# Seven block products for eight in the second MLP layer of a one-core encoder block

## The chip, the core and the metric

The kernel runs on one NeuronCore of one Trainium2 chip. The metric is the device time of one execution in microseconds (us): 1042.65 us before the change, the median of three runs (1041.05 to 1043.44). Times inside the kernel come from one profiled execution, counted from the first to the last instruction of the core. A difference of about 0.2% (2 us) is the least that a measurement of this kernel can tell from none.

The engines are named as in the profile: PE (TensorE) multiplies matrices and PEld is its weight load, DVE (VectorE) and ACT (ScalarE) work elementwise, POOL (GpSimd) works elementwise and issues DMAs, SP (SyncE) only issues DMAs. A matmul multiplies a stationary operand of up to 128x128 with a moving operand of up to 128x512 and adds into a bank of PSUM of 128 rows by 512 columns. SBUF is the core's on-chip memory.

## What is computed

One layer of a hybrid encoder for 512 tokens of 1024 numbers: three token mixers (gated convolution, RG-LRU, RWKV-7), a gated merge, an output projection, and then a two-layer MLP with a final normalisation. Only the MLP matters here (`rms_norm` divides each token by its root mean square and multiplies by a weight):

```python
h2 = rms_norm(x, norm2_g[l])
x = x + jnp.square(jax.nn.relu(h2 @ mlp_w1[l])) @ mlp_w2[l]
return rms_norm(x, final_g)
```

The first weight matrix is 1024 x 4096, the second 4096 x 1024. All inputs and outputs are float32.

## The kernel before

**Number format.** A matmul of the kernel takes operands of type fp32r (float32 of reduced precision). To keep float32's precision each operand is kept as two fp32r tiles: `hi`, the value cast to fp32r (ACT), and `lo`, the rest, `value - hi` (DVE). A product is three matmuls into one PSUM bank, written by `mm3` (L167): hi by hi, and the two mixed ones. The three have lines L168, L169 and L170 in the profile.

**Weights.** `load_w` (L133) loads one 128 x 1024 row tile of weights (512 KB) into a `raw` buffer by a DMA of SP (L136), then `split_w` makes `whi` (ACT, L147) and `wlo` (DVE, through the helper `tt`, L104). There are two `raw` buffers, and three each of `whi` and `wlo`. Everything in `load_w` has a priority that puts it ahead of its place in the code, so that weights are fetched and split early.

**First layer.** For each of the 32 row tiles `fi` of the hidden vector the loop at L978 multiplies the weights with `h2h`, `h2l` (the merged activations, 8 tiles of 128 x 512): 24 matmuls into one PSUM bank `p1`. ACT takes the relu into `r` (L983), DVE squares it, ACT casts it to `ah` (L991), DVE makes `al`. The root-mean-square factor of each token is not in there: squared relu lets it be taken out, so it is applied after the second layer. Beside the first two row tiles, `to_tokens` transposes the residual stream to token rows, writes it to the DRAM tensor `x2d` and collects each token's sum of squares in `ss2`.

**Second layer.** The eight PSUM banks hold the output, 4 tiles of 128 tokens by 2 halves of 512 columns (`acc`). For each row tile `fi`, `mlp2` adds, for each of the eight banks, the product of `ah`/`al` (128 tokens, stationary) and `whi`/`wlo` (512 columns, moving): 24 matmuls per row tile, 768 in all. The residual comes back from `x2d` in one DMA of 2 MB, issued by POOL together with the final norm's weights `fgt` (L1003, L1005) when the first layer's operands are free.

**End.** The last `NL` = 3 row tiles are done token tile by token tile, so that `last(i)` of one token tile runs beside the matmuls of the next: DVE scales the bank by the token's factor `sc2` and adds the residual (L1037, helper line L107), ACT squares and sums (L1039), a root (L1045) and a reciprocal give the final norm's factor, DVE and ACT scale the two halves, and SP and ACT issue the output DMAs.

**What sets the order.** Each engine runs its instructions in one fixed order. A scheduler makes it from the code's order and the priorities when the program is built; a buffer that is handed out again makes its writer wait for the last reader of the earlier use. No engine overtakes an instruction of its own that waits.

Of the kernel before, what the change touches and what calls it, by code (L numbers as in the profile page):

```python
# [18 lines left out]
P = 128  # L19
# [13 lines left out]
NL = 3  # L33
# [65 lines left out]
def block_kernel(ctx, tc, xt, win, par, mulr, sw, wout, w1, w2, fg, cst, eyes, out):  # L99
# [848 lines left out]

    fc = fill_chain()
# [10 lines left out]
    NA = 3 * NF // 4  # L960
    with tc.tile_pool(name="mw", bufs=2) as mw, \
            tc.tile_pool(name="ap", bufs=1) as apool, \
            ExitStack() as apool2:
        ahs = [apool.tile([P, NA, S], F32R, name="ah", align_bytes=ALM)]
        als = [apool.tile([P, NA, S], F32R, name="al", align_bytes=ALM)]
        ahl = lambda fi: (ahs[fi // NA][:, fi % NA], als[fi // NA][:, fi % NA])

        def mlp1(t, w, beside=None):
# [6 lines left out]
            if beside:  # L975
                drain(beside)

        for fi in range(NF):  # L978
            t = pp.tile([P, S], F32, tag="pp", name="p1")
            w = load_w(w1[fi])  # L980
            mlp1(t, w, to_tokens(fi) if fi < 2 else None)
# [3 lines left out]
            if fi == NA:  # L985
                xr_ctx.close()
                ap2 = apool2.enter_context(tc.tile_pool(name="ap2", bufs=1))
                ahs.append(ap2.tile([P, NF - NA, S], F32R, name="ah2", align_bytes=AL))
                als.append(ap2.tile([P, NF - NA, S], F32R, name="al2", align_bytes=AL))
            ahi, alo = ahl(fi)  # L990
            ac.copy(ahi, r)  # L991
            tt(alo, r, f(ahi), SUB)
# [3 lines left out]
        sc2 = cp.tile([P, 4], F32, name="sc2")  # L996
        tt(sc2, ss2[:, 0], ss2[:, 1], ADD)
        ts2(sc2, sc2, 1.0 / D, EPS, MUL, ADD)
        v.reciprocal(sc2, sc2)
        h2_ctx.close()  # L1000
        with tc.tile_pool(name="fin", bufs=1, side="right") as fin:
            xr = fin.tile([P, 4, D], F32, name="xr2")
            gp.dma_start(xr, x2d.rearrange("i p d -> p i d"))  # L1003
            fgt = fin.tile([P, D], F32, name="fgt")
            gp.dma_start(fgt, fg.to_broadcast([P, D]))  # L1005
            bank = lambda pool, tag: pool.tile([P, S], F32, tag=tag, name="acc")
            acc = [[bank(pc, "pu"), bank(pc, "pS")], [bank(pc, "py"), bank(pm, "pm")],
                   [bank(pm, "pm"), bank(pp, "pp")], [bank(pp, "pp"), bank(pp, "pp")]]

            def mlp2(fi, w, i, h):  # L1010
                ms = slice(i * P, (i + 1) * P)
                ahi, alo = ahl(fi)
# [4 lines left out]
            for fi in range(NF - NL):  # L1017
                w = load_w(w2[fi])
                for i in range(4):
                    for h in range(2):  # L1020
                        mlp2(fi, w, i, h)

            wl2 = [load_w(w2[fi]) for fi in range(NF - NL, NF)]

            def last(i):
# [3 lines left out]
                if i == 0:  # L1029
                    for d_ in range(NL - 1):  # L1030
                        for h in range(2):
                            mlp2(NF - NL + d_, wl2[d_], i, h)
                for h in range(2):
                    hs = slice(h * S, (h + 1) * S)
                    for d_ in range(NL - 1 if i == 0 else 0, NL):
                        mlp2(NF - NL + d_, wl2[d_], i, h)
                    stt(xr[:, i, hs], acc[i][h], sc2[:, i:i + 1], xr[:, i, hs], MUL, ADD)  # L1037
                    junk = fin.tile([P, S], F32, tag="fj", name="fj", bufs=2)
                    ac.activation(junk, xr[:, i, hs], AF.Square, accum_out=ss[:, h:h + 1])  # L1039
                    if h == 0:  # L1040
                        x0, x1 = xr[:, i, 0:S], xr[:, i, S:D]
                        o0 = x0 if i < 3 else fin.tile([P, S], F32, name="x3f")
                        (gp if i < 3 else v).tensor_tensor(out=o0, in0=x0, in1=fgt[:, 0:S], op=MUL)
                tt(sd[:, 0:1], ss[:, 0:1], ss[:, 1:2], ADD)
                ac.activation(sd[:, 1:2], sd[:, 0:1], AF.Sqrt, bias=epst[:, 0:1], scale=1.0 / D)  # L1045
                v.reciprocal(sd[:, 0:1], sd[:, 1:2])
                stt(x1, x1, sd[:, 0:1], fgt[:, S:D], MUL, MUL)
                sy.dma_start(out[i, :, S:D], x1)
                ac.activation(o0, o0, AF.Copy, scale=sd[:, 0:1])
                ac.dma_start(out[i, :, 0:S], o0)  # L1050

            for i in range(4):
                last(i)
# [75 lines left out]
```

## Time and profile before

| | before |
|---|---|
| time, median of 3 runs | 1042.65 us |
| span of the profiled execution, first to last instruction | 1039.6 us |
| granted TensorE clock, mean | 0.996 |
| first layer, first to last matmul start | 680.0 to 857.7 us |
| second layer, first to last matmul start | 857.9 to 1031.7 us |
| busy in the span: PE, PEld, DVE, ACT, POOL | 98%, 80%, 62%, 46%, 11% |
| DMA: moved, mean rate over the span | 145.23 MB, 140 GB/s |

The span is that of the one execution that was profiled; what lies around it (3.05 us to the median of the runs) is start and end of the program. The page gives each engine's busy time, the same in 40 slices of 26 us, the DMA queues, the chain of waits that ended last, and groups of equal instructions with their mean duration. Matmuls overlap by pipelining: one shows 389 ns from start to end, but the next begins some 0.23 us after it, and only that distance adds up to time.

### The profile page before, as it was taken

Reading aid. Unit: us, or ns where it says so; the run is one execution under the profiler, and the core shown is the slowest. Engines: PE = TensorE matmul, PEld = TensorE weight load, DVE = VectorE, ACT = ScalarE, POOL = GpSimd, SP = SyncE. Lnnn points to the kernel's source line nnn. Section 1 sums busy time; section 2 is a strip of 40 time slices with the busy share of each in tenths; the row PEclk is TensorE's granted clock in tenths of the full one; section 3 lists DMA queues with packets and bytes.
Section 4 is the critical chain, followed back from the end, with each engine's and each line's share of the span. In section 5 each row is a group of like instructions: output and inputs, shape, how many; then the busy total and the mean of one; then the engine's idle time right before and its main releaser. Section 6 shows DMA issues by size and latency. Waiting matters only on the chain. (4 is left out here: it accounts for less than half of the span.)

```text
span 1039.6 us, 15488 instructions
## 1 busy us (share of the span) xinstructions
PE 1021.4 (98%) x6180; PEld 831.5 (80%) x6180; DVE 648.4 (62%) x1087; ACT 480.6 (46%) x694; POOL 110.4 (11%) x180
## 2 busy tenths in 40 slices
PE   8999999999999999999999999999999999999997
PEld 5777877888878788888888778888888888888885
DVE  6997596599865875994567787564444442212224
ACT  7756453655544635556454444353443332221124
POOL 1013011202112112012222101010000000000001
PEclk9999999999999999999999999999999999999999
DMA  6344644734446346343997524443223335333232
GB/s 231 125 122 125 173 129 133 203 112 133 127 137 172 122 142 203 114 117 108 312 280 224 159 88 139 158 162 102 93 91 101 102 101 185 100 102 102 87 96 81
DMA packets 44504, 145.23 MB, mean 140 GB/s; under 512 B 6096, under 2 KB 9680, under 8 KB 43408
## 3 DMA queue, kind: packets, MB, share of 16 engines
q1 hardware_dynamic: 29472, 91.02, 27.6%
q0 software_dynamic: 14240, 52.18, 17.4%
q8 instruction: 48, 0.79, 0.3%
q10 hardware_dynamic: 720, 1.05, 0.3%
q14 instruction: 24, 0.20, 0.1%
HBM read 117.49 MB, written 26.74 MB: 139 GB/s over the span
## 5 line engine op out<-in xcount | busy, mean ns | idle before, releaser
L104 DVE TENSOR_TENSOR wlo<-raw,whi 128x1024 fp32r<-128x1024 f32 (+1 forms) x164 | 198.1, 1209 | 262.0 <-ACT whi L147 261.8
L147 ACT CAST whi<-raw 128x1024 fp32r<-128x1024 f32 (+1 forms) x164 | 170.0, 1037 | 320.8 <-PE acc L170 125.0
L168 PE MATMUL pp<-hh,whi 128*128 128x512 f32 x688 | 271.0, 394 | 0.4 <-DVE rs L107 0.4
L169 PE MATMUL pp<-hl,whi 128*128 128x512 f32 x688 | 270.1, 393 | 0.0
L170 PE MATMUL pp<-hh,wlo 128*128 128x512 f32 x688 | 269.2, 391 | 0.2 <-DVE wlo L104 0.2
L168 PEld LDWEIGHTS pp<-hh,whi 128*128 128x128 f32 x688 | 129.1, 188 | 28.8 <-DVE rs L107 0.8
L170 PEld LDWEIGHTS pp<-hh,wlo 128*128 128x128 f32 x688 | 129.2, 188 | 27.4 <-DVE wlo L104 0.6
L169 PEld LDWEIGHTS pp<-hl,whi 128*128 128x128 f32 x688 | 129.2, 188 | 26.3
L168 PE MATMUL p<-h2h,whi 128*128 128x512 f32 x256 | 100.4, 392 | 0.0
L170 PE MATMUL p<-h2h,wlo 128*128 128x512 f32 x256 | 99.7, 389 | 0.0
L169 PE MATMUL p<-h2l,whi 128*128 128x512 f32 x256 | 99.7, 389 | 0.0
L168 PE MATMUL acc<-whi,ah 128*128 128x512 f32 x256 | 99.6, 389 | 0.0
L169 PE MATMUL acc<-wlo,ah 128*128 128x512 f32 x256 | 99.6, 389 | 0.0
L170 PE MATMUL acc<-whi,al 128*128 128x512 f32 x256 | 99.6, 389 | 0.0
L170 PEld LDWEIGHTS p<-h2h,wlo 128*128 128x128 f32 x256 | 48.1, 188 | 10.1
L169 PEld LDWEIGHTS acc<-wlo,ah 128*128 128x128 f32 x256 | 48.1, 188 | 10.0
L170 PEld LDWEIGHTS acc<-whi,al 128*128 128x128 f32 x256 | 48.1, 188 | 9.9
L168 PEld LDWEIGHTS acc<-whi,ah 128*128 128x128 f32 x256 | 48.1, 188 | 9.9
L169 PEld LDWEIGHTS p<-h2l,whi 128*128 128x128 f32 x256 | 48.1, 188 | 9.7
L168 PEld LDWEIGHTS p<-h2h,whi 128*128 128x128 f32 x256 | 48.1, 188 | 9.6
L991 ACT CAST ah<-r 128x512 fp32r<-128x512 f32 x32 | 19.9, 623 | 43.3 <-DVE r L104 43.3
L104 DVE TENSOR_TENSOR al<-r,ah 128x512 fp32r<-128x512 f32 x32 | 22.1, 692 | 20.9 <-ACT ah L991 20.9
(308 smaller groups left out, 1343.7 us busy)
## 6 DMA issues: line engine op xcount, KB each, us to landing
raw<-in_win SPq DMA_DIRECT2D x88, 512.0 KB, 3.7
raw<-in_w SPq DMA_DIRECT2D x64, 512.0 KB, 3.5
ax<-axd POOLq DMA_DIRECT2D x8, 1024.0 KB, 9.6
axd<-AXt POOLq DMA_DIRECT2D x12, 512.0 KB, 7.4
bkd<-BKT POOLq DMA_DIRECT2D x4, 1024.0 KB, 14.0
raw<-in_wout SPq DMA_DIRECT2D x8, 512.0 KB, 3.6
bk<-bkd POOLq DMA_DIRECT2D x7, 512.0 KB, 11.8
swr<-in_sw SPq DMA_DIRECT2D x16, 128.0 KB, 2.9
```

The lines of the kernel that those rows point to most:

```text
L104: return v.tensor_tensor(out=o, in0=a, in1=b, op=op)
L147: ac.copy(hi[:, sl], raw[:, sl])
L168: pe.matmul(ps, wh, xh, start=start, stop=False)
L169: pe.matmul(ps, wh, xl, start=False, stop=False)
L170: pe.matmul(ps, wl, xh, start=False, stop=stop)
L991: ac.copy(ahi, r)
```

## The change

**Pairs.** Of the 32 row tiles of the second layer, 24 are taken as 12 pairs (`NPAIR`). A pair's contribution is a 2 x 2 block product: its two row tiles by the two halves of the tokens (256 each) on one side, its two row tiles by the two halves of the columns (512 each) on the other. Done directly it has eight block products. The new code uses Strassen's scheme in Winograd's form: seven block products, with sums and differences of blocks as operands. A block product is 6 matmuls (two token tiles by three). The 8 other row tiles stay as they were, grouped in four units of two.

**Stages.** The eight banks are now four pairs of banks `BX`, `BZ`, `BY`, `BW`, and the products come in three stages over the pairs, with weights loaded for each stage anew:
- Stage 1 (`prep1`): per pair one 512 KB load; DVE makes the difference `T` and two `wlo` halves, ACT two `whi` halves; 12 matmuls into `BX` and `BZ`. For the last 4 pairs (from `NPS` = 8 on) the activation operands are also split here (`a2`).
- Stage 2 (`prep2`): one 512 KB load; DVE makes `T` and `raw` anew, then `wlo`, `tl` and `a3l`, ACT `whi`, `th`, `a3h`; 18 matmuls into `BY`, `BW`, `BX`. Ahead of every third pair a unit of plain row tiles (`prep_plain`, one 512 KB load of two half rows) adds 24 matmuls.
- Stage 3 (`prep3`): two loads of 256 KB; DVE makes `raw` anew, `wlo`, `a2l`, ACT `whi`, `a2h`; 12 matmuls into `BZ` and `BX`. Ahead of every sixth pair a plain unit of 24. The last two units are done token tile by token tile, 12 matmuls each, with `finish(i)` in the place of `last(i)`.

Between the stages `fold` adds a finished bank to the residual tile `xr` (DVE); a bank may go on accumulating after a fold, so a value can be counted in several outputs. In all there are 696 matmuls, where there were 768.

**Token factor.** Since sums over different tokens are now formed, the factor must be in the activations. `token_roots` computes it from `ss2` (12 small DVE instructions), spreads it over the partitions with two matmuls beside row tile 3, and the relu becomes one DVE instruction `max(t, 0) * rsb` on PSUM, followed by a square on ACT. The first three row tiles wait for it in other PSUM banks. For a pair's row tiles DVE forms four sums of 128 x 256 at the end of the first layer, kept in `at2`, `at3`, `ATh`, `ATl`.

**Buffers and queues.** A third `raw` buffer is added; `T` uses the buffers of `r`, `one` and `ATh`; the splits of `a2`, `th`, `tl` use the eight `ATl` buffers, `a3` two of its own. The residual is now loaded by SP, in four DMAs of 512 KB between the weight loads, the final weights later in two.

The diff, cut to its core:

```diff
-NL = 3
+NL = 2
+NPAIR, NPS = 12, 8
...
+    def token_roots(o):
+        q = cp.tile([P, 3, 4], F32, name="rsq")
+        tt(q[:, 0], ss2[:, 0], ss2[:, 1], ADD)
+        ts2(q[:, 0], q[:, 0], 1.0 / D, EPS, MUL, ADD)
+        rsqrt(q[:, 0], q[:, 1], q[:, 2])
...
+        tt(dg, ident.unsqueeze(1).to_broadcast([P, 4, P]), q[:, 1].unsqueeze(2).to_broadcast([P, 4, P]), MUL)
...
+        ac.copy(hi, dg)
+        tt(lo, dg, f(hi), SUB)
+        for _ in range(5):
+            yield
+        pr = pm.tile([P, S], F32, tag="pm", name="rt")
+        pe.matmul(pr, ones_r, hi, start=True, stop=False)
+        pe.matmul(pr, ones_r, lo, start=False, stop=True)
+        ac.copy(o, pr)
...
+        def relu2_row(fi, t):
+            r = mw.tile([P, S], F32, tag="r", name="r")
+            stt(r, t, 0.0, rsb, MAX, MUL)
...
-            r = mw.tile([P, S], F32, tag="r", name="r")
-            ac.activation(r, t, AF.Relu)
-            tt(r, r, r, MUL)
...
-            gp.dma_start(xr, x2d.rearrange("i p d -> p i d"))
...
-            def mlp2(fi, w, i, h):
-                ms = slice(i * P, (i + 1) * P)
-                ahi, alo = ahl(fi)
-                hs = slice(h * S, (h + 1) * S)
-                mm3(acc[i][h], ahi[:, ms], alo[:, ms], w[1][:, hs], w[2][:, hs],
-                    start=fi == 0, stop=fi == NF - 1)
...
+            def prep1(p):
+                with tc.high_priority(offset=OFF):
+                    w = new_w2()
+                    sy.dma_start(w[0], w2[ev(p)])
...
+                    tt(TT_[p], w[0][:, H1], w[0][:, H0], SUB)
+                    ac.copy(w[1][:, H0], w[0][:, H0])
+                    tt(w[2][:, H0], w[0][:, H0], f(w[1][:, H0]), SUB)
+                    ac.copy(w[1][:, H1], TT_[p])
+                    tt(w[2][:, H1], TT_[p], f(w[1][:, H1]), SUB)
...
+            def prep2(p):
+                with tc.high_priority(offset=OFF):
+                    w = new_w2()
+                    sy.dma_start(w[0], w2[od_(p)])
+                    T = TT_[p]
+                    tt(T, w[0][:, H1], T, SUB)
+                    tt(w[0][:, H1], w[0][:, H0], T, SUB)
+                    split_w(w, slice(0, D))
+                    th, tl = spare([P, S], "th"), spare([P, S], "tl")
+                    ac.copy(th, T)
+                    tt(tl, T, f(th), SUB)
+                    return w, (th, tl), parts(AT[p][1], "a3", 3)
+
+            def prep3(p):
+                with tc.high_priority(offset=OFF):
+                    w = new_w2()
+                    sy.dma_start(w[0][:, H0], w2[od_(p)][:, H1])
+                    sy.dma_start(w[0][:, H1], w2[ev(p)][:, H1])
+                    tt(w[0][:, H1], w[0][:, H0], w[0][:, H1], SUB)
+                    split_w(w, slice(0, D))
+                    return w, parts(AT[p][2], "a2", 2)
...
+            for p in range(NP_):
+                w, a_ = prep1(p)
+                w0, w1_ = two(w)
+                if p % 2 == 0 and p // 2 < 4:
+                    sy.dma_start(xr[:, p // 2], x2d[p // 2])
+                prod(BX, a_[0], w0, p == NP_ - 1)
+                prod(BZ, a_[1], w1_, p == NP_ - 1)
```

**Where it moves instructions.** First place: DVE where the second layer begins. `p1_7885` is the last bank of the first layer, `wlo_7843` (before) and `wlo_7940` (changed) belong to the second layer's first weights. Before:

```order
L104 TENSOR_TENSOR wlo_7843<-raw_7841,whi_7842 128x1024
L104 TENSOR_TENSOR r_7742<-r_7742 128x512
L104 TENSOR_TENSOR al2_7564<-r_7742,ah2_7563 128x512
L104 TENSOR_TENSOR wlo_7873<-raw_7871,whi_7872 128x1024
L104 TENSOR_TENSOR r_7778<-r_7778 128x512
```

Now, from the first half of that weight's split on (`a3l_8269` is an operand of stage 2; `T_7942`, `T_7965`, `T_7987` are the differences of pairs 0, 1, 2):

```order
L105 TENSOR_TENSOR wlo_7963<-raw_7961,whi_7962 128x512
L108 SCALAR_TENSOR_TENSOR r_7916<-p1_7885,rsb2_6581 128x512
L105 TENSOR_TENSOR T_7942<-raw_7938 128x512
L105 TENSOR_TENSOR a3l_8269<-at2_0_7014,a3h_8268 128x768
L105 TENSOR_TENSOR wlo_7940<-T_7942,whi_7939 128x512
L105 TENSOR_TENSOR T_7965<-raw_7961 128x512
L105 TENSOR_TENSOR T_7987<-raw_7983 128x512
L105 TENSOR_TENSOR ATh_7880<-at3_11_7882,at2_11_7881 128x256
L105 TENSOR_TENSOR wlo_7985<-raw_7983,whi_7984 128x512
L105 TENSOR_TENSOR wlo_7963<-T_7965,whi_7962 128x512
```

Before, the second layer's first weights were split two row tiles ahead of the end of the first layer; now the second halves of pairs 0 and 1 stand behind the relu of the last row tile.

Second place: ACT and DVE in stage 2, where the third pair's operand `a3` is made (`raw_8388`, `T_8010`, `th_8396` belong to the fourth pair, `whi_8359`, `wlo_8360` to the plain unit ahead of it). ACT now:

```order
L148 CAST whi_8325<-raw_8324 128x1024
L148 CAST whi_8359<-raw_8358 128x1024
L1136 CAST th_8396<-T_8010 128x512
L1090 CAST a3h_8336<-at2_2_7174 128x768
L148 CAST whi_8389<-raw_8388 128x1024
```

DVE now:

```order
L105 TENSOR_TENSOR wlo_8326<-raw_8324,whi_8325 128x1024
L105 TENSOR_TENSOR T_8010<-raw_8388,T_8010 128x512
L105 TENSOR_TENSOR wlo_8360<-raw_8358,whi_8359 128x1024
L105 TENSOR_TENSOR raw_8388<-raw_8388,T_8010 128x512
L105 TENSOR_TENSOR a3l_8337<-at2_2_7174,a3h_8336 128x768
```

The third pair's `a3` stands behind the fourth pair's `T` on both engines, and so behind the load of `raw_8388`. Before, each engine had one instruction per row tile here, `whi` and `wlo`.

Third place: SP's queue at the start of the second layer. Before it held weights alone:

```order
L136 DMA raw_7841<-in_w2 128x1024
L136 DMA raw_7871<-in_w2 128x1024
L136 DMA raw_7901<-in_w2 128x1024
L136 DMA raw_7931<-in_w2 128x1024
L136 DMA raw_7961<-in_w2 128x1024
```

Now the residual's pieces `xr2` stand between them:

```order
L1113 DMA raw_7938<-in_w2 128x1024
L1113 DMA raw_7961<-in_w2 128x1024
L1113 DMA raw_7983<-in_w2 128x1024
L1113 DMA raw_8006<-in_w2 128x1024
L1169 DMA xr2_7929<-x2d_69 128x1024
L1113 DMA raw_8028<-in_w2 128x1024
L1113 DMA raw_8051<-in_w2 128x1024
L1113 DMA raw_8073<-in_w2 128x1024
L1169 DMA xr2_7929<-x2d_69 128x1024
```

The residual has moved from POOL's queue to SP's, behind the fourth, the seventh and later weights.

More of the change, by code (lines that the diff above doesn't have):

```diff
@@ L1017, in block_kernel @@
[L1017 to L1025, printed above, removed]
+            BX = [bank(pp, "pp"), bank(pp, "pp")]
+            BZ = [bank(pp, "pp"), bank(pm, "pm")]
+            BY = [bank(pm, "pm"), bank(pc, "pu")]
+            BW = [bank(pc, "pS"), bank(pc, "py")]
+            begun = set()
@@ new lines, in block_kernel, with prod @@
+            H0, H1 = slice(0, S), slice(S, D)
+            def prod(b, xs, ws, last=False, tiles=(0, 1)):
+                xh, xl = xs
+                wh, wl = ws
+                for i in tiles:
+                    ms = slice(i * P, (i + 1) * P)
+                    for n, (x_, w_) in enumerate(((xh, wh), (xl, wh), (xh, wl))):
+                        pe.matmul(b[i], x_[:, ms], w_, start=id(b[i]) not in begun, stop=last and n == 2,
+                                  skip_group_check=True)
+                        begun.add(id(b[i]))
@@ new lines, in two, with new_w2 @@
+            def two(w):
+                return (w[1][:, H0], w[2][:, H0]), (w[1][:, H1], w[2][:, H1])
+            nraw = [0]
+            def new_w2():
+                nraw[0] += 1
+                raw = fin.tile([P, D], F32, tag="raw", name="raw") if nraw[0] % 3 == 0 else \
+                    wp.tile([P, D], F32, tag="raw", name="raw", bufs=2)
+                return (raw,) + tuple(wp.tile([P, D], F32R, tag=t, name=t, bufs=3, align_bytes=AL)
+                                      for t in ("whi", "wlo"))
@@ new lines, in plain @@
+            def plain(u, w, b, th, last=False, tiles=(0, 1)):
+                ts_ = slice(th * HS, th * HS + HS)
+                for k, ws in enumerate(two(w)):
+                    prod(b, (ah[:, 2 * u + k, ts_], al[:, 2 * u + k, ts_]), ws, last and k == 1, tiles)
+            NU = NQ // 2
+            units = iter(range(NU))
+            for p in range(NP_):
[5 more added lines that the diff above has]
+                prod(BZ, a_[1], w1_, p == NP_ - 1)
@@ new lines, in block_kernel @@
+            with tc.high_priority(offset=OFF):
+                for i in range(2):
+                    fold(BX, i, i, H0)
+                    fold(BZ, i, 2 + i, H1)
+            for p in range(NP_):
+                if p % (NP_ // NU) == 0:
+                    u = next(units)
+                    w = prep_plain(u, H0)
+                    plain(u, w, BY, 0)
+                    plain(u, w, BW, 1)
+                w, t_, a_ = prep2(p)
+                w0, w1_ = two(w)
+                prod(BY, a_[0], w0, p == NP_ - 1)
+                prod(BW, a_[2], w1_, p == NP_ - 1)
+                prod(BX, a_[1], t_, p == NP_ - 1)
@@ L1027, in last, with finish @@
+            lastw = [prep_plain(u, H1) for u in range(done, NU)]
+            with tc.high_priority(offset=OFF):
+                for i in range(2):
+                    for hs in (H0, H1):
+                        fold(BX, i, 2 + i, hs)
+            def finish(i, b):
                 ss = fin.tile([P, 2], F32, tag="fss", name="fss", bufs=2)
                 sd = fin.tile([P, 2], F32, tag="fsd", name="fsd", bufs=2)
[L1029 to L1043, printed above, removed]
+                x0, x1 = xr[:, i, H0], xr[:, i, H1]
@@ L1052, in block_kernel @@
             for i in range(4):
-                last(i)
+                b = (BZ, BY)[i // 2]
+                for n, u in enumerate(range(done, NU)):
+                    plain(u, lastw[n], b, i // 2, n == NL - 1, (i % 2,))
+                finish(i, b[i % 2])
         ps.close()
```

141 lines of the change are left out of this document (117 added, 24 removed).

## The prediction

> **What bounds the kernel now.** I read the page from the top: busy shares, slices, then the chain of waits.
>
> ```profile
> span 1039.6 us, 15488 instructions
> PE 1021.4 (98%) x6180; PEld 831.5 (80%) x6180; DVE 648.4 (62%) x1087; ACT 480.6 (46%) x694; POOL 110.4 (11%) x180
> ...
> PE   8999999999999999999999999999999999999997
> ...
> DVE  6997596599865875994567787564444442212224
> ...
> PEclk9999999999999999999999999999999999999999
> DMA  6344644734446346343997524443223335333232
> GB/s 231 125 122 125 173 129 133 203 112 133 127 137 172 122 142 203 114 117 108 312 280 224 159 88 139 158 162 102 93 91 101 102 101 185 100 102 102 87 96 81
> ```
>
> PE is busy in every slice, the second layer's included (the last seven), and its clock is granted in full. DVE shows 2 to 4 tenths there, DMA 2 to 3. The windows by stage and the list for the tile `acc` (the second layer's banks) say it more closely:
>
> ```profile
> 858.00:1031.00 173.00, 173.00 (x765) 143.31 (x764) 46.44 (x47) 39.86 (x50) 5.32 (x5) 1.00 0.33 107
> L168 PE MATMUL acc<-whi,ah x256: 389/389/389, 857.9 to 1031.3; 128*128 128x512 f32 x128
> ...
> L170 PE MATMUL acc<-whi,al x256: 388/389/389, 858.3 to 1031.7; 128*128 128x512 f32 x128
> ```
>
> The first line has the columns PE, PEld, DVE, ACT, POOL (us and count), clock, DMA share, GB/s: PE 173.00 of 173.00, DVE 46.44. PE is never waiting in this stage, so what counts is the number of matmuls and the distance from one to the next, (1031.3 - 857.9) / 765 = 0.2267 us.
>
> **The change, part by part.** (1) Matmuls: 12 pairs, each 42 in place of 48, so 72 x 0.2267 = **16.3 us less**. (2) `token_roots` adds two: **+0.45 us**. It must be ready when PE comes to them, 36 matmuls (8.2 us) after row tile 1: DVE needs about 2.2 us for the weight split queued ahead, 12 small steps of 0.2 (0.17 each in the row below, and a handoff), then 0.7 + 0.6 + 0.7 for the diagonal, its cast and rest: 6.6 us. I take no wait; without that cover it would be up to 1 us. (3) The relu and the pair sums in the first layer: DVE needs for two row tiles 2 x 1.23 + 2 x 0.75 + 4 x 0.42 + 0.69 = 6.3 us in 10.9 us of PE. Hidden. All of these are from the lines by form of the stretch 640 to 1040 us (the small step from the list of tile `rqq`):
>
> ```profile
> L104 DVE TENSOR_TENSOR wlo<-raw,whi 128x1024 fp32r<-128x1024 f32 x69 | 84.5, 1225 | 189.4 <-ACT whi L147 189.3
> L147 ACT CAST whi<-raw 128x1024 fp32r<-128x1024 f32 x69 | 72.4, 1050 | 201.0 <-PE acc L170 125.0 <-PE p L169 56.7 <-PE acc L169 10.1
> L104 DVE TENSOR_TENSOR al<-r,ah 128x512 fp32r<-128x512 f32 x32 | 22.1, 692 | 20.9 <-ACT ah L991 20.9
> L991 ACT CAST ah<-r 128x512 fp32r<-128x512 f32 x32 | 19.9, 623 | 43.3 <-DVE r L104 43.3
> L107 DVE SCALAR_TENSOR_TENSOR xr<-acc,sc,xr 128x512 f32<-128x512 f32 x8 | 5.9, 747 | 2.4 <-PE acc L170 2.4
> L104 DVE TENSOR_TENSOR ym<-pYt,gq 128x256 f32<-128x256 f32 x3 | 1.3, 421 | 1.0 <-PE pYt L724 1.0
> L104 DVE TENSOR_TENSOR rqq<-rqq x27: 149/172/176, 19.7 to 363.8; 128x16 f32<-128x16 f32 x27
> ```
>
> (4) Does DVE keep up? Per pair, PE against DVE. Stage 1: 12 matmuls 2.72, three halves 2.08 (2.77 in the last four pairs). Stage 2: 18 matmuls 4.08; three halves, one full split and one of 768 columns (0.96, between 0.69 and 1.23) 4.26; with the plain unit (5.44 against 1.23) three pairs make 17.7 against 14.0. Stage 3: 2.72 against 0.69 + 1.23 + 0.69 = 2.61; with the unit six pairs make 21.8 against 16.9. DVE goes from a quarter to some 80% of PE's time: enough, but each late input now shows. So I walked the three orders shown above with these durations.
>
> (5) Start of the second layer: after PE's last first-layer matmul DVE does the relu 0.75, `T` 0.69, `a3l` 0.96, then the second half of `wlo` 0.69, with handoffs 3.3 us. PE has 10 matmuls of first halves and 3 of `whi` only, 2.95 us: 0.4 us wait. Pair 1's second half follows 3.2 us later (three of 0.69, one of 0.42, one of 0.69), PE meanwhile has 12 more matmuls, 2.7 us: 0.5 us. **+0.9 us**. (6) Stage 2, third pair: from the stage's start DVE has `tl`, `T`, four folds, a split, `raw`, `tl`, `T`, a split: 9 x 0.69 + 2 x 1.23 = 8.7 us; that split frees the `raw` buffer for the fourth pair's load, 3.5 us; then `T`, the plain split, `raw`, `a3l`: 0.69 + 1.23 + 0.69 + 0.96 = 3.6. Together 15.8 us, and PE needs it after 5.44 + 2 x 4.08 and one matmul more = 13.8. **+2.0 us**; later groups enter with all buffers filled, 0. (7) The end. Before, the last output was issued 3.8 us after the last matmul (start 1031.7, its 0.23 us over at 1031.95). The end of the chain in order of time, and the pieces by tile and form:
>
> ```profile
> 1032.05 1.43 DVE xr L107 x2
> ...
> 1033.50 0.73 ACT fj L1039 x2
> ...
> 1034.97 0.75 DVE xr L107
> L1039 ACT ACTIVATE fj<-xr 128x512 f32<-128x512 f32 x8 | 5.0, 631 | 7.1 <-DVE xr L107 7.0
> L1039 ACT ACTIVATION_READ_ACCUMULATOR fj<-xr 128x1 f32 x8 | 1.5, 186 | 0.0
> L1045 ACT ACTIVATE fsd<-fsd,epst x3: 279/280/294, 1027.5 to 1034.4; 128x1 f32<-128x1 f32 x3
> L1046 DVE RECIPROCAL fsd<-fsd x3: 164/164/165, 1027.8 to 1034.8; 128x1 f32<-128x1 f32 x3
> L1049 ACT ACTIVATE xr<-xr,fsd x2: 722/723/724, 1028.0 to 1032.1; 128x512 f32<-128x512 f32 x2
> ```
>
> Now ACT has at that point three squares with their sums (3 x 0.82), two roots (0.56) and a scaling (0.72) in its order ahead of the last reciprocal and scaling (0.16 + 0.75): some 0.4 us after the matmul it can begin, 4.9 to 5.2 in all. **+1.1 us**, between 0 and 1.4.
>
> (8) Loads. They take, from issue to landing (min/median/max): the first layer's; two of the proj stage issued 1.1 us apart; and the two beside the 2 MB residual load:
>
> ```profile
> L136 SPq DMA_DIRECT2D raw<-in_w x29: 327/328/328, 702.4 to 854.8; - x29
> ...
> DMA to landing us min/median/max: 3.4/3.5/3.7
> L136 SPq DMA_DIRECT2D raw<-in_win x2: 327/327/327, 348.0 to 349.1; - x2
> ...
> DMA to landing us min/median/max: 3.5/3.8/4.0
> L136 SPq DMA_DIRECT2D raw<-in_w x2: 327/328/328, 860.2 to 865.9; - x2
> ...
> DMA to landing us min/median/max: 5.2/6.3/7.4
> L152 SPq DMA_DIRECT2D raw<-in_win x1: 387/387/387, 0.7 to 0.7; - x1
> ...
> DMA to landing us min/median/max: 2.7/2.7/2.7
> ```
>
> In stage 3 DVE's order is `raw` of the next pair, then `wlo` of this one. So a load waits for the `wlo` of two pairs before, and two pairs take L + 0.69 + 1.23 + 0.1 us, where L is the time to landing. Two quarter-MB loads (2.7 for one, the second issued some 0.5 later) make L = 3.2 to 3.5, and 2.6 to 2.75 us per pair against PE's 2.72. It just fits. The residual's four pieces on SP add up to 1.4 us to the load behind them; three buffers in stage 1 give 8.2 us of PE time for L + about 3, so I cost them at 0 (at most 5.5). For a load that is a little late here and there I take **+0.7 us**, between 0 and 6.
>
> Sum: -16.3 + 0.45 + 0.9 + 2.0 + 1.1 + 0.7 = **-11.1 us**, so the span becomes 1028.5. The 3.05 us around it stay: **1031.5 us** from the median. With no wait and no longer end it would be 1026.8.
>
> The Trainium skill, page "DMA: Bandwidth & Descriptors", section "Latency and other measured facts", puts access to HBM at 0.2 us on average and 2 us at high load, and calls it the main part of a DMA's fixed cost. By that rule a stage that doubles its traffic would see loads 1.8 us slower, an estimate of 5.3 us; it is weighed as rival C. In this trace 5.2 came only beside 2 MB of other traffic.
>
> **The rivals.** A price for load time first: 44 weight loads pass three `raw` buffers, so where loads set the pace each us of L beyond about 3.6 costs 44 / 3 = 14.7 us.
> - B, loads set the pace in part. L is 4.0, the row of loads issued close together. 0.4 x 14.7 = 5.9 us more: 1037.4. For it: the stages ask for 512 KB per 2.72 us, 193 GB/s, where the row above has 107. Against: one slice on the page moved 312 GB/s.
> - C, **slower than before**: the same place, SP's loads of stages 1 and 3, at the 5.2 us of the row beside the residual: 1.6 x 14.7 = 23.5 us more, 1055. It decides from L = 3.6 + 11.1 / 14.7 = 4.36 us on. Against: that row has a second queue moving 2 MB at once; now the same bytes stand in line in SP's own queue.
> - D, the waits slow PE's clock. The trace shows it once:
>
> ```profile
> 4.00:8.00 4.00, 1.20 (x3) 0.12 (x2) 0.86 (x2) 2.24 (x5) 0.50 (x1) 1.00 0.86 263
> 8.00:12.00 4.00, 4.00 (x8) 2.04 (x8) 3.65 (x6) 3.98 (x8) 0.80 (x1) 0.57 1.05 383
> ```
>
> PE busy for 1.20 of 4 us, and in the next 4 us a clock of 0.57, so 1.7 us lost per such episode. My waits are 2.0 us at most, with PE busy around them. Three episodes would give 1036.6. [...]
> - E, the change doesn't do what it says: PE's order has 696 matmuls into these banks, so only their distance could differ (other tiles, other strides). At 0.232 each it would lose 3.7 us; 1035.2.
>
> **How the numbers follow.** Forecast 0.60 (1027 to 1036, with E and small forms of D in it); B and D 0.21 (1036 to 1040); waits that eat the gain to within 0.2% (2.1 us, 1040.5 to 1044.8; about what a measurement of this kernel can tell from no change) 0.10; C 0.09. Faster 0.81, same 0.10, slower 0.09. The range takes the forecast's case and B: 1027 to 1040, with 0.19 outside.
>
> **What would show it.** PE's distance still 0.2267 in all stages (1); 0.45 us for two `rt` matmuls with no gap ahead (2); gaps of PE ahead of the second halves of the first two pairs, released by DVE `wlo` (5); one gap of some 2 us near 14 us into stage 2, released by `a3h`/`a3l` (6); 5 us from the last matmul to the last output's issue (7); loads of 3.4 to 3.7 us to landing and PE gaps of less than 1 us in stage 3 (8). The prediction is wrong if loads land at 4.4 us or later in the median, if DVE's halves take clearly more than 0.69 us beside ACT and POOL, or if gaps recur in each group of stage 2.

## The result, and the profile after

| | before | changed |
|---|---|---|
| median of the timed runs | 1043.05 us (4 runs, 1041.05 to 1044.2) | **1029.58 us** (4 runs, 1028.16 to 1030.43) |
| ratio | 1 | **0.9872**, 95% interval 0.9856 to 0.9887 |
| span of the profiled execution | 1039.6 us | 1027.7 us |
| first matmul of the first layer | 680.01 us | 681.98 us |
| first layer, first matmul to first of the second layer | 177.87 | 178.89 |
| second layer, first to last matmul | 173.85 | 159.16 |
| start of the last matmul to the end of the span | 7.83 | 7.69 |

The medians are 13.5 us apart, the forecast was 11.1 (1031.5 from 1042.65), its range 1027 to 1040. In the profiles the two layers and the end together are 13.8 us shorter, and the changed program comes to the first layer 2.0 us later, in a part of which the change touches only one cast and the places of tiles in memory.

Most of these 2.0 us probably come from which execution of before was profiled. A later profile of the same kernel (`control`, below) has the same span, 1039.6 us, and begins the first layer at 679.98 us; the time of that execution was 1041.39 us, less than the median of 1043.05. If the layers take equally long in every execution, the median one begins the first layer near 681.6 us (an estimate: 1043.05 less the 361.4 us between those two figures), 0.3 us or so ahead of the changed kernel's 681.98. Then 13.8 less 0.3 are the 13.5 us of the medians. For the same reason the 3.05 us that were put down to start and end of the program are too many: where a run lists the time and the span of one execution, they are 1.7 to 2.2 us apart.

The page of the changed kernel, the same lines as before:

```profile
span 1027.7 us, 15699 instructions
PE 1007.2 (98%) x6110; PEld 817.7 (80%) x6110; DVE 735.1 (72%) x1251; ACT 512.9 (50%) x757; POOL 110.1 (11%) x179
...
PE   8999999999999999999999999999999999999997
...
DVE  6997497599865886794668779656554546887775
...
PEclk9999999999999999999999999999999999999999
DMA  6444643734546446434897724544333325644442
```

PE is still at 9 tenths in the second layer, at full clock. DVE went there from 2 tenths in most slices to 7 or 8, DMA from 2 or 3 to 4 to 6. The windows from the first layer's first matmul to the second's, and from there to its last matmul (columns: PE, PEld, DVE, ACT, POOL in us and count, clock, DMA share, GB/s), of before:

```profile
680.01:857.88 177.87, 177.87 (x801) 147.32 (x800) 86.44 (x107) 74.10 (x112) 4.39 (x8) 1.00 0.34 107
857.88:1031.73 173.85, 173.85 (x768) 144.00 (x767) 47.12 (x47) 40.71 (x52) 5.32 (x5) 1.00 0.33 106
```

and of the changed kernel:

```profile
681.98:860.87 178.89, 178.56 (x804) 147.59 (x802) 94.78 (x147) 67.92 (x110) 4.38 (x8) 1.00 0.32 100
860.87:1020.03 159.16, 158.44 (x697) 130.12 (x695) 125.64 (x170) 78.92 (x113) 5.18 (x4) 1.00 0.48 161
```

DVE's work in the second layer rose from 47 to 126 us, 79% of the layer, and PE stayed busy for 158.4 of 159.2 us. What PE waited for there is one line in the view of its waits, and its place is in the chain of work that ended last (start, us, what):

```profile
PE acc L1076 <- DVE a3l L105: 0.7, 1, 0.7
```

```profile
894.71 0.60 DVE T L105
895.31 2.39 DVE xr L105 x4
897.71 1.13 DVE wlo L105
...
901.94 3.52 DMA raw<-in_w
905.46 0.02 issue
905.48 0.06 DVE T L105
905.54 0.55 issue
906.09 1.22 DVE wlo L105
907.31 0.60 DVE raw L105
907.91 0.88 DVE a3l L105
908.79 0.04 issue
908.83 1.20 PE acc L1076 x4
```

Read it from the end: PE takes up the third pair of stage 2 when `a3l` is there; that stood behind `raw` and a split, these behind the load into `raw`, and the load behind DVE's queue with the four foldings into `xr`. It is the wait that the prediction had as step 6, at its place. In PE's order of time the matmuls there start at 907.62 and 908.83, and the next 0.34 later: 1.1 us lost in place of 2.0.

### The profile page after: what moved, and what is told of

Its sections match the earlier page's. It is cut to its first block, busy times and chain, and to the rows that moved or that the text cites. A ratio compares the mean times of both kernels' runs of the same rounds, so it can differ in the third digit from the quotient of the medians.

```text
span 1027.7 us, 15699 instructions
## 1 busy us (share of the span) xinstructions
PE 1007.2 (98%) x6110; PEld 817.7 (80%) x6110; DVE 735.1 (72%) x1251; ACT 512.9 (50%) x757; POOL 110.1 (11%) x179
## 5 line engine op out<-in xcount | busy, mean ns | idle before, releaser
L105 DVE TENSOR_TENSOR wlo<-raw,whi 128x1024 fp32r<-128x1024 f32 (+1 forms) x176 | 206.5, 1175 | 91.2 <-ACT whi L148 90.6
L108 DVE SCALAR_TENSOR_TENSOR r<-p,rsb 128x512 f32<-128x512 f32 x32 | 22.0, 691 | 69.3 <-PE p L171 68.8
L171 PEld LDWEIGHTS p<-h2h,wlo 128*128 128x128 f32 x256 | 48.1, 188 | 10.2
L1225 POOL TENSOR_TENSOR x0f<-xr,fgt 128x512 f32<-128x512 f32 x4 | 5.2, 1296 | 310.6 <-DMA raw<-in_w 301.4
L170 PE MATMUL acc<-ml,whi 128*128 128x512 f32 x64 | 25.0, 391 | 0.0
L171 PE MATMUL acc<-mh,wlo 128*128 128x512 f32 x64 | 25.0, 390 | 0.0
L1076 PE MATMUL acc<-whi,a2h 128*128 128x512 f32 x64 | 24.9, 389 | 0.0
L1076 PE MATMUL acc<-whi,a2l 128*128 128x512 f32 x64 | 24.9, 389 | 0.0
L1076 PE MATMUL acc<-wlo,a2h 128*128 128x512 f32 x64 | 24.9, 389 | 0.0
L1076 PE MATMUL acc<-whi,ah 128*128 128x512 f32 x64 | 24.9, 389 | 0.0
```

The lines of the kernel that those rows point to most:

```text
L105: return v.tensor_tensor(out=o, in0=a, in1=b, op=op)
L108: return v.scalar_tensor_tensor(out=o, in0=a, scalar=s, in1=b, op0=op0, op1=op1)
L170: pe.matmul(ps, wh, xl, start=False, stop=False)
L171: pe.matmul(ps, wl, xh, start=False, stop=stop)
L1076: pe.matmul(b[i], x_[:, ms], w_, start=id(b[i]) not in begun, stop=last and n == 2, skip_group_check=True)
L1225: gp.tensor_tensor(out=o0, in0=x0, in1=fgt[0], op=MUL)
```

## The experiments

Where a layer's length is given, it is from first matmul to first or last matmul, as in the table. Each set of runs has its own runs of before, with medians from 1041.8 to 1043.13 us; a ratio is to those, so times of different sets are best compared by their ratios.

**eight: is it the count of matmuls?**

```diff
+                prod(BX, a_[1], t_)
                 prod(BX, a_[1], t_, p == NP_ - 1)
```

> Issues the third product of each pair of stage 2 (bank BX) twice: 72 matmuls more, so as many as eight products per pair have, with every load, split, buffer and order of the changed kernel kept. The product counts twice in the output. Theory (the gain is the count of matmuls at 0.2267 us each): 16.3 us more than the changed kernel, less up to 1.1 us since PE then comes later to the third pair of stage 2 and waits less there; 1029.6 + 15.2 to 16.3 = 1044.8 to 1045.9 us, ratio to before 1.002 to 1.003. Rival (part of the gain comes from other loads, buffers or the new order, and the matmuls themselves are partly hidden): well below that, under 1041 us; or, if DVE or loads set the pace of stage 2, less than 10 us more than the changed kernel.

1047.01 us, ratio to before 1.0048 (1.003 to 1.0065).

```profile
862.91:1037.52 174.61, 174.42 (x769) 143.71 (x767) 126.28 (x170) 79.88 (x113) 5.19 (x4) 1.00 0.45 146
```

With 72 matmuls put back the second layer takes 174.61 us, 15.45 more than with the change and 0.76 more than before: the other loads, the splits and the new order cost PE only that, and the wait at the third pair is gone (PE now comes to it later). The time itself came out 1.1 us above the range, since this program, too, was late at the first layer, at 684.4 us; that part is taken up below. The gain is the count.

**token_only: what the token factor costs.** The kernel before with the new relu and `token_roots` alone:

```diff
+            stt(r, t, 0.0, rsb, MAX, MUL)
+            ac.activation(r, r, AF.Square)
...
-            ac.activation(r, t, AF.Relu)
-            tt(r, r, r, MUL)
+            if fi == 2:
+                roots = token_roots(rsb)
...
-        sc2 = cp.tile([P, 4], F32, name="sc2")
...
-                    stt(xr[:, i, hs], acc[i][h], sc2[:, i:i + 1], xr[:, i, hs], MUL, ADD)
+                    tt(xr[:, i, hs], acc[i][h], xr[:, i, hs], ADD)
```

> The kernel before with one part of the change alone: the token factor is taken into the relu of the first layer (two matmuls and twelve small DVE steps for it), and the last steps lose their factor; the second layer has its 768 matmuls. Theory: this part costs the first layer 0.45 us for two matmuls and up to 0.6 us of waiting, so its length goes from 177.9 to 178.3 to 178.9 us; the end loses nothing. Time 1043.0 to 1044.2 us, ratio 1.0000 to 1.0012. Rival (the relu by DVE and the roots ahead of row tile 2 make PE wait in the first layer, or the loads behind them come late): 2 to 4 us more than before.

1045.18 us, ratio 1.0026 (1.0014 to 1.0039), more than the theory allowed. But not in the layers:

```profile
686.20:864.81 178.61, 178.61 (x804) 147.52 (x802) 90.64 (x118) 76.35 (x114) 4.39 (x8) 1.00 0.35 106
864.81:1038.66 173.85, 173.85 (x768) 143.96 (x767) 46.50 (x49) 41.07 (x53) 5.33 (x5) 1.00 0.33 106
```

The first layer is 0.74 us longer without any idle time of PE, the second the same, the end 0.6 us shorter. That is +0.1 us in sum. The rest lies ahead of the first layer, which begins at 686.2 us in the profile. That execution was the slowest of nine (1047.65 us); in the median, 2.4 us above before's 1042.76, some 2.3 us lie there, an estimate from these two numbers. So the rival's time came, but not by waits in the first layer.

**two_raw: what the third buffer is worth.**

```diff
-                raw = fin.tile([P, D], F32, tag="raw", name="raw") if nraw[0] % 3 == 0 else \
-                    wp.tile([P, D], F32, tag="raw", name="raw", bufs=2)
+                raw = wp.tile([P, D], F32, tag="raw", name="raw", bufs=2)
```

> The changed kernel without the third raw buffer, two for all 44 loads of the second layer. By the prediction's formula for a buffer (time to landing plus what DVE and ACT need until it is read, some 3.5 + 2.5 us in stage 1, 2.9 + 0.7 + 1.2 in stage 3, 3.5 + 3 in stage 2, divided by two buffers): 3.0 us per pair in stage 1 against 2.72 of PE, 3.25 against 4.08 in stage 2, 2.5 to 2.75 against 2.72 in stage 3: 3 to 6 us more than the changed kernel, with the gaps of PE in stage 1 and at the plain units. Rival (loads never set the pace; the third buffer is only reserve): less than 1 us. Second rival (each us of load time is paid for by 44/3 us, as the prediction's price had it): over 12 us.

1040.7 us, ratio 0.9976 (0.9963 to 0.999). The second layer takes 168.36 us, 9.2 more, and the end 1.4 more. PE's waits there:

```profile
PE acc L1076 <- DVE wlo L105: 3.2, 4, 2.0
PE acc L1076 <- ACT whi L1117: 1.3, 1, 1.3
PE acc L1076 <- DVE a3l L105: 0.7, 1, 0.7
PE acc L1076 <- ACT whi L1119: 0.5, 1, 0.5
PE acc L1076 <- ACT whi L148: 0.4, 1, 0.4
```

All three forecasts missed: less than 1 and 3 to 6 us were too little, 12 or more too much. Every wait in the list (6.1 us; the rest are smaller gaps that it leaves out) is for an operand that ACT or DVE had still to split, and behind the splits of weights the chain shows loads of 3.5 to 5.3 us. So the loads, with the splits that free their buffers, do set the pace as soon as one buffer is missing: the 10.6 us are three quarters of the change's gain.

**xr_pool: loads that are really late.**

```diff
+            gp.dma_start(xr, x2d.rearrange("i p d -> p i d"))
...
-                if p % 2 == 0 and p // 2 < 4:
-                    sy.dma_start(xr[:, p // 2], x2d[p // 2])
```

> The changed kernel with the residual's 2 MB as one DMA on POOL's queue, as before the change, in place of four pieces on SP's queue between the loads. Loads of stage 1 beside it should take 5 to 7.5 us to landing (5.2 and 7.4 in the profile of before). Theory (three buffers leave a load some 5 us without a wait of PE): 0 to 2 us more than the changed kernel, as gaps in the first 15 us of the second layer. Rival (the prediction's price, 14.7 us for each us of load time over the whole layer, so 1.2 us for each pair's load that is 3 us late): 3.5 us or more.

1033.71 us, ratio 0.9918 (0.9903 to 0.9933). The list for the load of stage 1, in the changed kernel and then here:

```profile
L1113 SPq DMA_DIRECT2D raw<-in_w x12: 327/328/328, 841.5 to 880.1; - x12
...
DMA to landing us min/median/max: 3.4/4.5/5.8
```

```profile
L1114 SPq DMA_DIRECT2D raw<-in_w x12: 327/328/328, 842.6 to 885.3; - x12
...
DMA to landing us min/median/max: 3.4/4.3/8.4
```

In the changed kernel loads of stage 1 took 4.5 us in the median and up to 5.8, and PE waited 0.4 us in all. Here three loads took 8.0 to 8.4 us, and PE lost 4.1 us in the first 15 us of the layer, in two gaps of 1.45 and 1.28 us where those loads landed and in smaller ones beside them. The wait at the third pair was gone, so the layer is 161.82 us, 2.66 more. That lies between theory and rival, with loads later than either had them; the time, 4.1 us more, would fit the rival, but 1.65 us of it lie ahead of the first layer. Three loads, some 4.7 us each beyond 3.5, cost 3.7 us more than was lost in the changed kernel: 0.26 us for each us of one load, where the prediction's price (14.7 us for 44 loads) is 0.33. For loads this late the price nearly holds; smaller delays, those of the changed kernel, cost next to nothing.

**skip: has DVE room in stage 2?**

```diff
-                prod(BX, a_[1], t_, p == NP_ - 1)
+                if p == NP_ - 1:
+                    prod(BX, a_[1], t_, True)
```

> The changed kernel without the third product of stage 2 (bank BX) for 11 of 12 pairs: 66 matmuls fewer, 15.0 us of PE; the output lacks these products. Every load, split and difference is still made. In stage 2 a group of three pairs then costs PE 13.6 us (5.44 + 3 x 2.72) and DVE 14.0 us by the prediction's sums, 12.6 by the distances of 0.60 and 1.14 us at which DVE's instructions follow each other in the profile. Theory (instructions queued on DVE follow at 0.60 and 1.14, so DVE has room that the prediction did not see): 13 to 15 us less than the changed kernel. Rival (DVE and the loads are at their limit in stage 2): 10 us less or fewer, with a gap of PE in each group released by a3l or tl.

1019.39 us (4 runs, 1017.36 to 1025.26), ratio 0.9792 (0.9759 to 0.9825); the second layer 146.65 us, 12.5 of the 15.0 us less.

```profile
PE acc L1076 <- DVE a3l L105: 1.9, 1, 1.9
PE acc L1076 <- ACT a3h L1090: 0.5, 1, 0.5
```

Both waits are at the third pair again (PE now comes there earlier). At the same place in the next two groups of three pairs PE loses 0.2 and 0.35 us more (matmuls at 922.08 and 936.04 us, both released by `a3l`), and in the last group nothing. So the rival's sign is there, but small: the layer's 12.5 us lie between the two forecasts, and the time, 10.2 us less, at the rival's bound, with runs that spread over 8 us. With PE at 13.6 us for three pairs DVE nearly keeps up. Its rows say why:

```profile
906.09 1.22 DVE L105 TENSOR_TENSOR wlo<-raw,whi 128x1024 fp32r<-128x1024 f32 x1
907.22 0.95 DVE L105 TENSOR_TENSOR a3l<-at,a3h 128x768 fp32r<-128x768 f32 x1
908.09 0.68 DVE L105 TENSOR_TENSOR raw<-raw,T 128x512 f32<-128x512 f32 x1
908.69 0.69 DVE L105 TENSOR_TENSOR tl<-T,th 128x512 fp32r<-128x512 f32 x1
```

Instructions of 1.22, 0.95 and 0.68 us start 1.13, 0.87 and 0.60 us apart when they stand in the queue one behind the other: each begins 0.08 us before its predecessor's record ends. A sum of durations therefore overstates a full queue by about a tenth.

**fold_late: the third pair.**

```diff
-            with tc.high_priority(offset=OFF):
+            with tc.high_priority(offset=0):
                 for i in range(2):
                     fold(BX, i, i, H0)
                     fold(BZ, i, 2 + i, H1)
```

> The changed kernel, with stage 1's four foldings into xr queued later on DVE, behind the work for the first two pairs of stage 2 in place of ahead of it. Theory (the wait of PE at the third pair of stage 2, 1.1 us in the profile, comes from DVE's queue: the foldings stand ahead of the split that frees the buffer for that pair's load): the gap near 48 us into the second layer is gone or under 0.4 us, the second layer 0.7 to 1.1 us shorter, with no new gap, since the banks that are folded are not written again before 8 us into stage 2; time 1028.5 to 1029. Rival (the load itself is what is late there, or the bank's next product now waits for the folding): a gap of about 1 us stays there or appears at the first product into BX of stage 2; 1029.5 to 1031.

1027.68 us, ratio 0.9881 (0.985 to 0.9912). The second layer:

```profile
859.26:1017.38 158.12, 158.12 (x697) 130.23 (x695) 125.69 (x170) 78.87 (x113) 5.18 (x4) 1.00 0.48 162
```

The wait at the third pair is gone (what PE still loses is 0.45 us in the layer's first 5 us), and the layer is 1.04 us shorter, so the cause of that wait was the order of DVE's queue. In the runs' times a difference of 1 us does not stand out: 1027.68 us is below the forecast, the ratio no better than the changed kernel's 0.9872.

**pairs14: more of the same.** 28 row tiles in pairs, 12 matmuls fewer:

```diff
-NPAIR, NPS = 12, 8
+NPAIR, NPS = 14, 8
...
-                if p % (NP_ // NU) == 0:
+                if (p * NU) % NP_ < NU:
...
-                if p % (NP_ // (NU - NL)) == 0:
+                if (p * (NU - NL)) % NP_ < NU - NL:
```

> The changed kernel with 14 pairs (28 of 32 row tiles) in place of 12: 12 matmuls fewer, two plain units fewer in stage 2 and 3 each. Theory (PE's count still sets the time, DVE's cover in stages 1 and 3 is enough): 12 x 0.2267 = 2.7 us less than the changed kernel, 1026.9 (1026 to 1028) us. Rival (the plain units, 5.44 us of PE for 1.2 us of DVE, are what lets DVE and the loads catch up; with half as many PE waits in stages 2 and 3): no gain or a loss, 1029.5 to 1035 us.

1029.7 us, ratio 0.9878 (0.9856 to 0.9901): no gain in the time. That is the rival's figure, but hardly by its waits: the second layer is 157.20 us, 1.96 less of the 2.72, with waits of 2.1 us in place of 1.5, again at the third pair (`a3l`). In the profiled execution the first layer began at 685.0 us, later than in the changed kernel by more than was gained.

**control, before_ones, fold_ones, aligned: why the first layer begins late.** Between 485 and 545 us lies a stretch in which the RWKV scan's operands are loaded (DMA share 0.9 in the windows below), and there the profiles of changed programs lose time. I first asked whether it is chance, and then whether it comes from the order of the first microseconds, which the new cast of `ones_r` alters.

> The kernel before, unchanged, for a second profile of it. In every profile so far of a kernel with the changed relu the first layer begins 2.0 to 6.2 us later than in the one profile of before (680.0 us), though what stands ahead of it differs only in the order of the first some 15 us. Theory (that is the spread of single executions: the first 20 us, and waits for small DMAs near 500 to 525 us of the order of 10 to 15 us): here the first layer begins anywhere between 680 and 686 us, and the layers' own lengths repeat within 0.2 us (177.9 and 173.9). Rival (the change itself moves the part ahead): it begins at 680.0 within 0.5 us.

1041.39 us, the first layer at 679.98 us: the rival's figure. But this is one execution, below the median of before in its set (1041.8 us), and the first profile has the same span; two such do not show that before always begins there.

```diff
+            if fi == 2:
+                ones_r = cp.tile([P, P], F32R, name="ones_r")
+                ac.copy(ones_r, one.to_broadcast([P, P]))
```

> The kernel before, with nothing added but the cast of a tile of ones on ACT (128x128, read by nobody), which the change brings with the token factor. The order puts it in the first microseconds, and squares, casts and matmuls of the first 15 us change places; all work from there to the first layer keeps its order. The two profiles of before begin the first layer at 680.0 us, the eight of kernels that have this cast at 680.9 to 686.2. Theory (the new order of the first 15 us shifts the phase in which loads and small DMAs meet near 500 to 525 us, and costs 1 to 3 us there): 1 to 3 us more than before, first layer from 681 on, ratio 1.001 to 1.003. Rival (those shifts are chance of single executions): the same as before within 0.6 us.

1042.75 us, ratio 1.0003 (0.9984 to 1.0022). No cost, though the first layer came at 681.62 us, 1.6 us later, all of it lost in the first 22 us and none near 500. The profiled execution took 1042.97 us, close to the median.

```diff
-        ac.copy(ones_r, one.to_broadcast([P, P]))
+        ts2(ones_r, q[:, 0, 0:1].to_broadcast([P, P]), 0.0, 1.0, MUL, ADD)
```

> The changed kernel with the late foldings, and with the tile of ones written on DVE from the token sums (times 0, plus 1), so that it can't be written before the first layer: the first 15 us keep the order of before. Theory (the cast among the first instructions costs 1 to 3 us near 500 to 525 us): first layer from about 680 us on, its length 178.4 and the second layer's 158.1 as with the late foldings, so 1025 to 1027 us, 15 to 17 us less than before. Rival (chance of single executions): the same as with the late foldings alone, about 1027.5, the first layer anywhere between 680 and 686.

1029.31 us, ratio 0.9874 (0.9857 to 0.9892); the first layer at 683.27 us, 3.3 us of it lost between 485 and 545 us with the first microseconds in the order of before. So that theory fell as well. The edit above and the next are made to fold_late. What was left was where the tiles lie:

```diff
-        q = cp.tile([P, 3, 4], F32, name="rsq")
+        q = cp.tile([P, 5, 4], F32, name="rsq")
```

> The kernel with the late foldings, instruction for instruction, with one small tile of the token sums 32 bytes longer, so that all tiles behind it in the buffer memory lie 32 bytes further. The change had moved them by 544 bytes: the tiles into which POOL's queue loads the scan's operands at 490 to 545 us (ax, sv, tc, bk, rt) then begin at an odd multiple of 32 bytes, where in the kernel before, and in the one with the idle cast alone (moved by 512), they begin at a multiple of 64. That stretch is full of DMA (share 1.03), and from 485 to 545 us the ten profiles with the 544 bytes lose 1.3 to 4.9 us against before, those at multiples of 64 -0.1 and +0.4. Theory (those transfers are slower at odd multiples of 32 bytes): the stretch from 485 to 545 us as in before within 0.5 us, first layer from 680 to 682 us, time 2 to 3 us less than the late foldings with the 544 bytes, 1024.5 to 1026. Rival (chance, or another cause that came with the token factor): 1.3 us or more lost there again, time 1027 to 1029.

1029.65 us (6 runs, 1027.62 to 1034.99), ratio 0.9885 (0.9864 to 0.9907). The windows of that stretch, one row each of before, token_only, the changed kernel, fold_ones, before_ones and aligned:

```profile
485.00:545.00 60.00, 59.97 (x735) 48.57 (x735) 37.56 (x59) 31.68 (x45) 17.01 (x29) 1.00 0.92 272
```

```profile
485.00:545.00 60.00, 55.51 (x712) 45.05 (x708) 34.92 (x55) 27.11 (x38) 15.79 (x27) 1.00 0.90 239
```

```profile
485.00:545.00 60.00, 58.05 (x709) 47.00 (x709) 36.51 (x58) 29.65 (x43) 16.63 (x29) 1.00 0.93 258
```

```profile
485.00:545.00 60.00, 57.01 (x679) 46.01 (x679) 36.02 (x56) 29.28 (x41) 16.13 (x28) 1.00 0.91 265
```

```profile
485.00:545.00 60.00, 60.00 (x777) 48.72 (x776) 37.47 (x59) 31.04 (x45) 16.45 (x29) 1.00 0.87 268
```

```profile
485.00:545.00 60.00, 60.00 (x777) 48.92 (x771) 37.90 (x59) 31.07 (x44) 16.92 (x29) 1.00 0.91 263
```

In the profiled executions PE loses nothing where the tiles begin at multiples of 64 bytes (before, before_ones, aligned; the control 0.4), and comes 1.3 to 4.9 us later to the same matmul in all ten with the odd multiples of 32 (its idle time in the windows is 1.3 to 4.5 us). That is the split which the theory gave, and the one edit that moves the tiles back moved the loss to zero. But the times do not bear it out: 1029.65 us (ratio 0.9885) is no better than the 1027.68 of fold_late (0.9881), where 2 to 3 us less was forecast. One profile per kernel shows the stretch; that of aligned is of the fastest of six runs, which spread over 7 us. Whether the address costs time in the mean stays open.

**p14_ones: all together, and worse.** The edits of pairs14, fold_late and fold_ones in one kernel.

> The kernel with the tile of ones written late and the late foldings, and 14 pairs in place of 12: 12 matmuls fewer. With 14 pairs and early foldings the second layer took 157.2 us, of them 2.1 us of waits. Theory (the foldings are what delays the third to fifth pair of stage 2): waits fall to under 1 us, second layer 155.5 to 156.5, time 1 to 2.7 us less than the same with 12 pairs. Rival (with two plain units in place of four, DVE is behind in stage 2 whatever the order): waits of 2 us stay, second layer 157 us or more, time within 1 us of that with 12 pairs.

1032.39 us, ratio 0.9901 (0.9886 to 0.9916). The second layer took 160.99 us, 3.8 more than in pairs14. PE's order of time, and the windows around it:

```profile
910.35 0.39 PE L1076 MATMUL acc<-whi,a3l 128*128 128x512 f32 x1
913.63 0.64 PE L1076 MATMUL acc<-th,a3h 128*128 128x512 f32 x1 [2.89 <-DVE xr L105]
914.07 0.63 PE L1076 MATMUL acc<-th,a3l 128*128 128x512 f32 x1
914.50 0.63 PE L1076 MATMUL acc<-tl,a3h 128*128 128x512 f32 x1
```

```profile
910.00:914.00 4.00, 1.11 (x5) 0.62 (x4) 4.00 (x6) 1.31 (x2) 0.00 (x0) 0.98 0.21 20
914.00:918.00 4.00, 4.00 (x12) 3.13 (x11) 3.85 (x6) 1.35 (x2) 0.00 (x0) 0.59 0.74 244
```

With two plain units fewer the late foldings come too late: the third product of a pair writes the bank that has still to be folded, and PE waited 2.89 us for `xr`. Neither theory nor rival had this wait. Then its matmuls ran 0.43 us apart for some 3.5 us, at a clock of 0.59 in the second window. The order that helped 12 pairs hurts 14.

No version tried here beats the change by more than the runs can tell; fold_late is shorter by 1.0 us in its second layer, in the profile.

## Why the prediction was right, and where it was not

- **(1) The count.** 72 matmuls at 0.2267 us: right. 695 distances of 0.2267 are 157.6 us, and the waits found in the layer (1.5 us) fill it up to 159.16; eight gave it back.
- **(2) The two matmuls of `token_roots`,** +0.45 us. The first layer grew by 0.5 to 0.74 us in eight of the eleven profiles with them, and by 1.0 us in three (the changed kernel among them, where PE's busy time in the row above is 0.33 us short of the layer: a gap ahead of a transpose). No wait ahead of the two `rt` matmuls: the cover of 36 matmuls was enough. What the layer grew beyond 0.45 us is not explained.
- **(3), (4) DVE's cover.** Right: 125.6 of 159.2 us is the 80% of the forecast.
- **(5) Start,** +0.9: 0.4 in the profile (matmuls at 863.21 to 863.55 and 865.29 to 865.63 at distances of 0.30 to 0.34). The size was too large and the releaser was another: DVE's `wlo` was forecast, and both gaps end with a `whi` of ACT, the first with the second half of the first pair (863.16), the second with a first half whose load, issued at 861.06, had only just landed (864.54). **(6) Third pair,** +2.0: 1.1. The place, the releaser and the order were right; the size was off by the 0.08 us that successive DVE instructions overlap, some dozen of them in that chain. PE needed it 13.8 us after the stage's start, as forecast; DVE had it at 14.8 and not at 15.8.
- **(7) The end,** +1.1: -0.14. This step's term failed. It put "three squares with their sums" on ACT behind the last matmul (started 1020.03):

```profile
1019.06 0.63 ACT L1227 ACTIVATE fj<-xr 128x512 f32<-128x512 f32 x1
...
1019.69 0.62 ACT L1224 ACTIVATE fj<-xr 128x512 f32<-128x512 f32 x1
...
1021.25 0.29 ACT L1229 ACTIVATE fsd<-fsd,epst 128x1 f32<-128x1 f32 x1 [0.85 <-DVE fsd L105]
1021.45 0.61 ACT L1227 ACTIVATE fj<-xr 128x512 f32<-128x512 f32 x1
...
1023.24 0.72 ACT L1233 ACTIVATE x0f<-x0f,fsd 128x512 f32<-128x512 f32 x1 [0.29 <-DVE fsd L1230]
```

  Two of the three were ready and began before it, and ACT then even stood idle for 0.85 us. The order of a queue says what stands ahead, not when it can run.
- **(8) Loads,** +0.7: 0 in stage 3, where no gap of PE is left (the first quarter MB took 2.4 to 3.1 us). From the Trainium skill's page "DMA: Bandwidth & Descriptors", section "Latency and other measured facts", the prediction had worked out an estimate of 5.3 us for a load under high load. Stage 1's took 4.5 us in the median and 5.8 at most, so somewhat over half of the added time came, and almost none of what it was feared to cost. That 5.2 us came only beside 2 MB of other traffic is too narrow: in the trace of before the load issued at 551.0 us landed after 5.4 us while POOL's queue moved 0.88 MB, and the one issued at 320.6 after 12.4 us beside 2.1 MB.
- **Rivals.** C's load times came (4.5 us in the median in stage 1, beyond its 4.36) and its price did not: by it stage 1's twelve loads alone would have cost (4.5 - 3.6) x 12 / 3 = 3.6 us, and 0.4 was measured. The prediction also named 4.4 us in the median as a sign that it is wrong; in stage 1 that sign came, and the time was in the range all the same. A price by buffers holds only once the reserve is used up; two_raw shows it used up. D's slow clock came in a second layer in p14_ones alone, behind a wait of 2.89 us (in the prediction's two rows PE had been idle for 2.80 us); the waits of the changed kernel, 1.1 us at most, did not bring it. E fell: the distance is unchanged.

So the forecast for the layers and the end was -11.1 where the profile has -13.8, too careful by 0.5 (5), 0.9 (6), 1.24 (7) and 0.7 (8), and short by 0.6 in (2). That the profiled span (-11.9) fits it better is chance: the 2.0 us ahead of the first layer were in no step of it. The medians, -13.5, lie near the layers' sum.

## What to carry to other kernels

When PE is never waiting, a cheaper algorithm pays by its count of matmuls, and what remains to be found out is whether the engine that does the extra sums and the loads that feed it keep a reserve: here a third buffer of half a MB was worth 10.6 of 13.8 us. Price a late load only beyond that reserve, and follow what each wait stands behind: moving four foldings in DVE's queue removed one wait with 12 pairs and made a larger one with 14. Compare profiles stage by stage before crediting a difference of 2 us to a change, and look where in the spread of the runs each profiled execution lies.

## What the runs showed of the hardware

- DVE instructions that are queued start 0.60 us apart at a recorded 0.68, 1.13 at 1.22, 0.87 at 0.95.
- After 2.89 us without work (starts 3.28 us apart) PE's clock was 0.59 in the next 4 us; in finer windows of p14_ones it was 0.50 from 913.84 to 917.25 us and 1.00 on both sides. The trace of before has the same at its start: PE idle for 2.80 us up to 7.88, then 0.50 from 8.20 to 11.61. Gaps with starts 2.37 us apart (two_raw) and 2.34 (skip) left the clock at 1.00. The Trainium skill, page "TensorE: Matmul & The Clock Gate", section "HAM oscillation — how this bites in real kernels", puts the limit at about 3.4 us; by these two traces a gap can be shorter than that and still be followed by a slow clock.
- In single profiles, tiles at odd multiples of 32 bytes went with 1.3 to 4.9 us of PE's time in one stretch where the DMA engines were 0.87 to 0.94 busy; moving the tiles by 32 bytes, with the same instructions, took the loss away in the one profile of it. It was not confirmed in the times.
